# Turning the attention stages' tiles through the vector engine and DRAM instead of the matrix engine, on one Trainium2 core

## The chip, the cores and the metric

The kernel runs on one core of a Trainium2 chip. Five engines work on their own instruction streams: PE (matrix multiplication, with its weight loads shown as PEld), DVE (element-wise work and 32x32 block transposes), ACT (activations and copies), POOL (here powers and the issue of some DMAs) and SP (the issue of most DMAs). The metric is the device time of one execution in microseconds (us); several executions of the same program are compared by their median.

## The reference

One decoder layer over 256 tokens of width 2048, all in float32:

```
h = h + 1/2 * SwiGLU_1(RMSNorm(h))                 # d_ff = 5632
n = RMSNorm(h); P = n @ W_in                       # columns split among head groups
   A: retention, 8 heads of 128 (rotary, decay matrix, per-head GroupNorm, swish gate)
   B: sliding-window attention, 16 query heads on 2 key heads of 64, window 128, rotary, sinks
h = h + concat(A, B) @ W_out
h = h + CrossAttn(RMSNorm(h), RMSNorm(mem))        # 4 heads of 512 into 256 memory tokens
h = h + 1/2 * SwiGLU_2(RMSNorm(h))
out = RMSNorm(h)
```

A sliding head sees, for queries of the first 128 tokens, 128 keys (early groups, t = 0); for those of the second 128 tokens, 256 keys (late groups, t = 1). Softmax has one learned sink per head in its denominator.

## The kernel before

**The stream of weights.** Nearly all of PE's work is `x @ W` for large W. Every weight matrix is cut into `Unit`s (512 output columns, some 256) and each unit into steps. A step is 1024 weight values per partition: two blocks of 128 rows by 512 columns. `split` makes of a float32 weight piece `wf` a rounded part `wh` (ACT, line 71) and the rest `wl` (DVE, line 76), a pair that the text calls a split or halves; `three` (lines 468 to 470) multiplies with three matmuls, high by high, low by high and so on. For two token halves and two row blocks a step has 12 matmuls. All units stand in one list, `all_steps()` makes the order of steps, and `run_stream` writes them out one after another; units with `then` set are interleaved, so that each one's last row block comes after the others.

**Its lead.** At step c, `prepare(at + 1 + LOOKAHEAD)` writes the split of step c + 3, and `fetch(... + AHEAD)` the loads of four steps more. `wf` has three buffers of two steps, `wh` and `wl` have four each.

**Work beside the stream.** Everything else is a task with a due time: `later(delay, fn)` puts it `delay` steps after the current one, and tasks due are written into the program ahead of the split of that step. Each task's instructions stay behind what PE, ACT and DVE have already been given. So a unit's `done` function runs after its last step, and what it starts follows at fixed numbers of steps. `SWA_EVERY = 5` spaces the sliding-head groups, `TURN = 6` is the time of an exchange.

**Two ways to turn a tile.** PE can transpose 128x128 (a matmul with the identity `ident`) into a PSUM tile `tmp` (four of one bank), from which ACT and DVE make the halves. The other way is `cross`: DVE transposes 32x32 blocks of two 128x512 tiles into a `t4k` tile (two buffers), SP writes it to a DRAM `box` one step later, POOL reads it back with the blocks exchanged in four DMAs two steps after the start, and after six steps the function given to it uses the turned tile. In the kernel before, `cross` serves the feed-forward activations, the retention's queries and keys, all outputs that are added to h, and the memory attention's queries and keys.

**The mixer**, in the order of its units: sliding keys and values (`skv`, 4 steps), sliding queries (`sq`, two units of 8), then for each half g of the retention heads queries, keys (`rqk`), values (`rv`) and gate (`rg`), 8 steps each, then four units of `w_out` over the four blocks of `mixT`: blocks 0 and 1 are the retention's, 2 and 3 the sliding heads'. It is followed by the memory attention's keys, queries, values and output, four units each.

In the mixer before, PE turns: the keys (line 597), the queries (line 694, high and low parts side by side), each group's probabilities five steps after its scores (line 644), the gated retention output (line 334) and, later, the memory attention's probabilities (line 901). A sliding-head group (`swa_group`) is four early or two late heads. Its scores take one matmul per head against the keys' high and low halves side by side (line 618), and two DVE instructions add them with scale and mask (lines 623, 624). Then come maximum, exponential (ACT, line 633), sum and product (line 637). `swa_values` (four steps after the probabilities' halves) multiplies with the values and writes its part of `mixT` 2 and 3.

## Time and profile before

| | |
|---|---|
| three runs | 2184.91, 2185.42, 2190.97 us; median 2185.42 |
| profiled execution | 2186.15 us, its span from first to last instruction 2184.4 |
| granted PE clock | 0.999 |
| DVE, ACT, POOL busy | 1290.9, 1028.1, 135.4 us |
| moved by DMA | 472.00 MB, mean 216 GB/s |

In a row of the profile, `L644 PE MATMUL tmp<-ident,t2k 128*128 128x128 f32 x48 | 7.2, 272 | 0.0` is a line of the kernel, the engine, the operation, output and inputs by their names in the program, shapes and count; then busy us, mean ns of one, and the engine's idle time ahead of them with what ended it. In a timeline a row begins with start and duration in us. Matmuls overlap in PE's pipeline, so that the length of one is more than it takes from the stream; the distance from start to start shows the latter.

### The profile page before, as it was taken

The page shows a single profiled execution, that of the slowest core. Times are in us where ns is not written, and L with a number is a line of the kernel's source. Part 1 is how long each engine was busy: PE and PEld are TensorE (multiplying, and loading weights), DVE is VectorE, ACT ScalarE, POOL GpSimd, SP SyncE. Part 2 cuts the span into 40 slices and gives each one's busy share as a digit, 9 for nine tenths or more (in the row PEclk, how much of TensorE's full clock was granted, in tenths as well). Part 3 has the DMA queues.
Part 4 walks back from the last instruction along what each step waited for, and adds up shares of the span by engine and source line. Part 5 has one row for each costly group of instructions (what it writes and reads, how often), then busy time and mean ns, then how long its engine had stood idle before and what let it go on. Part 6 is the DMA issues. An engine that isn't in the chain of part 4 may idle for free.

```text
span 2184.4 us, 25213 instructions
## 1 busy us (share of the span) xinstructions
PE 2171.3 (99%) x9844; PEld 1803.3 (83%) x9844; DVE 1290.9 (59%) x1536; ACT 1028.1 (47%) x1258; POOL 135.4 (6%) x233
## 2 busy tenths in 40 slices
PE   9999999999999999999999999999999999999998
PEld 7888888888888888888888888888888888888886
DVE  6555555555556678786765555575555544555554
ACT  6444444444445555544654444455444433444443
POOL 0000000000000000000111000010101000000000
PEclk9999999999999999999999999999999999999999
DMA  7666677666667656556777655585768655666664
GB/s 270 231 218 216 212 231 225 218 212 227 216 224 254 216 175 199 179 183 205 269 238 246 216 174 174 202 258 201 256 232 255 214 193 193 212 211 213 221 212 145
DMA packets 134745, 472.00 MB, mean 216 GB/s; under 512 B 11233, under 2 KB 12001, under 8 KB 134497
## 3 DMA queue, kind: packets, MB, share of 16 engines
q1 hardware_dynamic: 123968, 441.88, 58.5%
q0 software_dynamic: 10368, 28.33, 5.5%
q8 instruction: 77, 1.26, 0.2%
q14 instruction: 44, 0.35, 0.0%
q10 hardware_dynamic: 288, 0.18, 0.0%
HBM read 439.93 MB, written 30.41 MB: 215 GB/s over the span
## 4 chain that ended last, share of the span: by engine, by line
PE 95%; DVE 2%; issue 2%; DMA 1%; ACT 0%; POOL 0%; SPq 0%; POOLq 0%; ACTq 0%; DVEq 0%
PE acc L469 31%; PE acc L468 31%; PE acc L470 31%; DVE wl L76 1%; PE tmp L470 0%; PE tmp L469 0%; PE tmp L468 0%; DMA t4k<-box 0%; DMA wf<-in_ffn_w_up 0%; PE tmp L618 0%; PE tmp L644 0%; ACT wh L71 0%; POOL t4k L455 0%; PE tmp L740 0%; DVE t4k L446 0%
## 5 line engine op out<-in xcount | busy, mean ns | idle before, releaser
L76 DVE TENSOR_TENSOR wl<-wf,wh 128x1024 fp32r<-128x1024 f32 (+1 forms) x776 | 942.2, 1217 | 789.9 <-ACT wh L71 787.1
L71 ACT ACTIVATE wh<-wf 128x1024 fp32r<-128x1024 f32 (+1 forms) x776 | 817.5, 1055 | 983.8 <-PE acc L470 947.2
L468 PE MATMUL acc<-wh,blk 128*128 128x512 f32 (+1 forms) x3104 | 1207.3, 389 | 2.3 <-ACT blk L71 2.3
L469 PE MATMUL acc<-wl,blk 128*128 128x512 f32 (+1 forms) x3104 | 1205.4, 388 | 0.4 <-DVE wl L76 0.4
L470 PE MATMUL acc<-wh,blk 128*128 128x512 f32 (+1 forms) x3104 | 1204.7, 388 | 0.0
L468 PEld LDWEIGHTS acc<-wh,blk 128*128 128x128 f32 x3104 | 582.9, 188 | 122.3 <-ACT blk L71 2.9
L470 PEld LDWEIGHTS acc<-wh,blk 128*128 128x128 f32 x3104 | 582.8, 188 | 120.4 <-DVE blk L356 0.4
L469 PEld LDWEIGHTS acc<-wl,blk 128*128 128x128 f32 x3104 | 582.9, 188 | 119.9 <-DVE wl L76 1.8
L455 POOL DMA_DIRECT2D t4k<-box x216 | 124.7, 584 | 1759.9 <-DMA box<-t4k 1034.6
L446 DVE STREAM_TRANSPOSE t4k<-t2k 128x512 f32<-128x512 f32 x76 | 49.3, 687 | 13.9 <-ACT t2k L71 13.9
L71 ACT ACTIVATE blk<-t4k 128x512 fp32r<-128x512 f32 (+1 forms) x68 | 39.1, 623 | 34.0 <-DMA t4k<-box 34.0
L76 DVE TENSOR_TENSOR blk<-t4k,blk 128x512 fp32r<-128x512 f32 x60 | 38.7, 687 | 14.5 <-ACT blk L71 14.4
L505 ACT ACTIVATE t2k<-acc,n 128x512 f32<-128x512 f32 x44 | 27.9, 686 | 31.2 <-PE acc L470 31.2
L71 ACT ACTIVATE blk<-tmp 128x512 fp32r<-128x512 f32 (+2 forms) x53 | 23.9, 458 | 25.0 <-DVE blk L76 19.6
L512 DVE SCALAR_TENSOR_TENSOR t2k<-acc,n,t2k 128x512 f32<-128x512 f32 x44 | 31.0, 746 | 6.4 <-PE acc L470 6.4
L71 ACT ACTIVATE blk<-h,gains 128x256 fp32r<-128x256 f32 x64 | 27.3, 496 | 1.5 <-DVE h L479 1.4
L356 DVE SCALAR_TENSOR_TENSOR blk<-h,gains,blk 128x256 fp32r<-128x256 f32 x64 | 26.8, 477 | 0.0
L76 DVE TENSOR_TENSOR blk<-tmp,blk 64x256 fp32r<-64x256 f32 (+2 forms) x45 | 22.1, 494 | 5.2 <-ACT blk L71 5.1
L393 DVE TENSOR_TENSOR t2k<-t2k,t2k 128x512 f32<-128x512 f32 x35 | 24.0, 687 | 1.5 <-ACT t2k L389 0.3
L479 DVE TENSOR_TENSOR h<-h,t4k 128x512 f32<-128x512 f32 x32 | 20.6, 685 | 4.1 <-DMA t4k<-box 4.1
L468 PE MATMUL tmp<-blk,blk 128*128 128x256 f32 (+1 forms) x80 | 22.6, 282 | 0.0
L469 PE MATMUL tmp<-blk,blk 128*128 128x256 f32 (+1 forms) x80 | 22.5, 282 | 0.0
(125 smaller groups left out, 460.3 us busy)
## 6 DMA issues: line engine op xcount, KB each, us to landing
wf<-in_ffn_w_down SPq DMA_DIRECT2D x88, 1024.0 KB, 4.8
wf<-in_ffn_w_gate SPq DMA_DIRECT2D x87, 1024.0 KB, 5.1
wf<-in_ffn_w_up SPq DMA_DIRECT2D x87, 1024.0 KB, 5.5
box<-t4k SPq DMA_DIRECT2D x54, 512.0 KB, 3.2
t4k<-box POOLq DMA_DIRECT2D x216, 128.0 KB, 5.1
wf<-in_w_in_rqk SPq DMA_DIRECT2D x16, 1024.0 KB, 5.1
wf<-in_w_in_rvg SPq DMA_DIRECT2D x16, 1024.0 KB, 5.2
wf<-in_w_out SPq DMA_DIRECT2D x16, 1024.0 KB, 5.0
```

Source lines behind the costliest of these rows:

```text
L71: return nc.scalar.activation(dst, src, AF.Copy, **kw)
L76: nc.vector.tensor_tensor(lo, src, hi, ALU.subtract)
L356: nc.vector.scalar_tensor_tensor(x[:, k, 1, :], v[:, k, :], g, x[:, k, 0, :], ALU.mult, ALU.subtract)
L393: nc.vector.tensor_tensor(self.sums, self.sums, y, ALU.add)
L446: nc.vector.transpose(z[:, t, :].rearrange("p (g q j) -> p q g j", g=4, q=4), squares_of(v))
L455: nc.gpsimd.dma_start(z[32 * g : 32 * g + 32].rearrange("p t (i n) -> p (t i) n", i=4), far[g])
L468: nc.tensor.matmul(o, ah, bh, start=start, stop=False)
L469: nc.tensor.matmul(o, ah, bl, start=False, stop=False)
L470: nc.tensor.matmul(o, al, bh, start=False, stop=stop)
L479: nc.vector.tensor_tensor(v, v, out[t], ALU.add)
L505: nc.scalar.activation(gated[b][t], acc[:, t, :], AF.Silu, scale=norm.scale(t))
L512: nc.vector.scalar_tensor_tensor(s[t], acc[:, t, :], norm.scale(t), s[t], ALU.mult, ALU.mult)
```

## The change

- The queries, the sliding heads' and the memory attention's probabilities and the gated retention output go through `cross` instead of PE. Only the keys are still turned by PE. The helper `turn` and the rounded identity `identr` are gone.
- The sliding queries are rotated into two `t2k` tiles and exchanged; the halves are made after the exchange (one pair for each token half and each of even and odd heads) and the high part lies on partitions 0 to 63 of `q`, the low on 64 to 127, as before.
- Sliding-head groups of one kind go in pairs: `swa_pair` runs two groups five steps apart, and the second one starts an exchange of both probability tiles. The values follow three (or four) steps after it.
- For late groups, the products with the keys' high and low halves are accumulated in PSUM (two matmuls of 256 columns per head), and one DVE instruction adds scale and mask.
- The retention's halves are made per token half and block of 128 columns, with the gain.
- The memory's norm blocks start from the second gate unit instead of the first `w_out` unit; `w_out` takes its blocks in the order 0, 2, 3, 1, and its first two units are interleaved.

```diff
-    def swa_group(g, t, heads, q, probs):
+    def swa_group(g, t, heads, q):
...
-        for b in range(2):
+        if t == 1:
+            ps = tmp_ps().rearrange("p (n k) -> p n k", n=nh)
+            for n in range(nh):
+                for c in range(2):
+                    nc.tensor.matmul(
+                        ps[:, n, :], q[:, heads[n], P:], st["k"][:, g, c, :], start=c == 0, stop=c == 1
+                    )
+            mask = ctab[:, C_MASK : C_MASK + S].rearrange("p (o k) -> p o k", o=1).broadcast_to([P, nh, S])
+            nc.vector.scalar_tensor_tensor(sv3, ps, 64 ** -0.5, mask, ALU.mult, ALU.add)
+        for b in range(0 if t == 1 else 2):
...
-        def second():
-            tp = tmp_ps()
-            for n in range(4):
-                nc.tensor.transpose(tp[:, n * P : (n + 1) * P], s[:, n * P : (n + 1) * P], ident)
...
-        later(5, second)
+        return s
+
+    def swa_pair(g, t, groups, q):
+
+        ss = []
+
+        def group(heads):
+            ss.append(swa_group(g, t, heads, q))
+            if len(ss) == 2:
+                cross(ss, second)
+
+        def second(out):
+            x = blk().rearrange("p k c s -> p k (c s)").rearrange("p k (n s) -> p k n s", n=4)
...
+            if t == 0:
+                for j in range(2):
+                    later(3 + j, lambda j=j: swa_values(g, t, groups[j][-1] // 4, pairs[j : j + 1]))
+            else:
+                later(3, lambda: swa_values(g, t, groups[0][-1] // 4, pairs))
+
+        for heads in groups:
+            st["swa_at"] = max(st.get("swa_at", 0) + SWA_EVERY, clock[0] + 1)
+            later(st["swa_at"] - clock[0], lambda heads=heads: group(heads))
...
     def sq_done(g):
         def done(acc):
...
-            z = blk().rearrange("p k c s -> p (k c s)").rearrange("p (t n c d) -> p t n c d", t=2, n=8, c=2)
             q = blk().rearrange("p k c s -> p (k c) s")
+            rs = [t2k() for _ in range(2)]
...
-            later(5, lambda: turned(0))
-            later(6, lambda: turned(1))
+            def turned(out):
+
+                for t in range(2):
+                    for odd in range(2):
+                        hi, lo = (
+                            q[64 * c : 64 * c + 64, odd::2, t * P : (t + 1) * P].rearrange("p n (a j) -> p n a j", a=4)
+                            for c in range(2)
+                        )
+                        halves(hi, lo, out[t][64 * odd : 64 * odd + 64])
+                swa_pair(g, 0, (range(0, 4), range(4, 8)), q)
+                for b in range(2):
+                    swa_pair(g, 1, (range(4 * b, 4 * b + 2), range(4 * b + 2, 4 * b + 4)), q)
+            cross(rs, turned)
...
-            def turned():
-                tp = turn(lambda t, kk: ret[t][:, kk * P : (kk + 1) * P])
-                mixT[g] = split_turned(tp, G_GN + 4 * g)
-            later(3, turned)
+            def turned(out):
+                x = blk()
+                for t in range(2):
+                    for k in range(4):
...
+                        copy(hi, out[t][:, k], scale=g1)
+                        nc.vector.scalar_tensor_tensor(lo, out[t][:, k], g1, hi, ALU.mult, ALU.subtract)
+                mixT[g] = x
+            cross(ret, turned)
+            if g == 1:
+                for b in range(4):
+                    later(4 + 4 * b, lambda b=b: mem_block(b))
...
-    to_h(a["w_out"], mixT, 1.0, (2, 3, 0, 1), None, out_done)
+    to_h(a["w_out"], mixT, 1.0, (0, 2, 3, 1), None, out_done)
+    units[-4].then = units[-3]
...
-        def probs():
-            tq = tmp_ps()
...
-        later(3, probs)
+        def probs(out):
+            w = blk().rearrange("p k c s -> p k (c s)")
...
+        if i % 2 == 0:
+            st["p"] = p
+        else:
+            cross([st["p"], p], probs)
```

## The prediction

> **What bounds the kernel now.** I read the page's busy times and its chain first, then the matrix engine's groups with shapes kept apart, then the starts of single instructions around the transposes, and last the vector engine where it is fullest.

> ```profile
> span 2184.4 us, 25213 instructions
> PE 2171.3 (99%) x9844; PEld 1803.3 (83%) x9844; DVE 1290.9 (59%) x1536; ACT 1028.1 (47%) x1258; POOL 135.4 (6%) x233
> PEclk9999999999999999999999999999999999999999
> PE 95%; DVE 2%; issue 2%; DMA 1%; ACT 0%; POOL 0%; SPq 0%; POOLq 0%; ACTq 0%; DVEq 0%
> ```

> PE is busy for 99% of the span at full clock and is 95% of the chain that ended last. Every instruction in PE's stream is therefore time, and what leaves the stream is gained unless PE then waits for something. The instructions that the change takes out are these (mean ns is of one, overlapped):

> ```profile
> L644 PE MATMUL tmp<-ident,t2k 128*128 128x128 f32 x48 | 7.2, 272 | 0.0
> L618 PE MATMUL tmp<-blk,blk 128*128 128x512 f32 x16 | 5.2, 408 | 0.0
> L694 PE MATMUL tmp<-identr,blk 128*128 128x128 f32 x32 | 3.2, 244 | 0.0
> L901 PE MATMUL tmp<-ident,t2k 128*128 128x128 f32 x16 | 2.4, 271 | 0.0
> L334 PE MATMUL tmp<-ident,t2k 128*128 128x128 f32 x16 | 2.1, 272 | 0.0
> ```

> L644 turns the sliding heads' probabilities, L694 their queries, L901 the memory attention's probabilities, L334 the retention output: 48 + 32 + 16 + 16 = 112 transposes. L618 makes the scores and stays.

> **What leaves PE.** A transpose's 272 ns is latency. What it takes from the stream is read from the chain (start, us, what) and from the starts of neighbouring instructions:

> ```profile
> 769.87 0.23 PE acc L469
> 776.91 0.64 PE tmp L694 x8
> 780.36 0.47 PE tmp L618 x4
> 795.17 0.47 PE tmp L618 x2
> 795.63 0.44 PE tmp L644 x4
> 899.97 0.87 PE tmp L334 x8
> 1273.10 0.44 PE tmp L901 x4
> ```
> ```profile
> 795.47 0.60 PE L644 MATMUL tmp<-ident,t2k 128*128 128x128 f32 x4
> 795.83 0.48 PE L468 MATMUL acc<-wh,blk 128*128 128x512 f32 x1
> 796.14 0.40 PE L469 MATMUL acc<-wl,blk 128*128 128x512 f32 x1
> ```

> By the chain: 12 x 0.44 + 4 x 0.64 + 2 x 0.87 + 4 x 0.44 = 5.3 + 2.6 + 1.7 + 1.8 = 11.4 us. By starts, four L644 take 0.36 (795.47 to 795.83), and the next matmul's gap is 0.31 instead of 0.23. Where a score group stands just ahead, that 0.08 may stay, so the lower end is 12 x 0.36 + 6.1 = 10.4. I take 10.7, since most L644 groups run behind L618. The late scores (16 matmuls of 512 columns, 0.47 for two) become 32 of 256 columns (0.47 for four): no change. Nothing is added to PE's stream.

> [...]

> **What is added to DVE.** Twelve new exchanges (2 of queries, 6 of probability pairs, 2 of retention, 2 of memory attention), each with two block transposes:

> ```profile
> 942.65 1.31 DVE L446 STREAM_TRANSPOSE t4k<-acc 128x512 f32<-128x512 f32 x2
> 943.99 0.69 DVE L76 TENSOR_TENSOR t2k<-tmp,t2k 128x512 fp32r<-128x512 f32 x1
> 944.60 0.74 DVE L623 SCALAR_TENSOR_TENSOR t2k<-tmp,ctab 128x256 f32<-128x256 f32 x2
> 945.26 0.74 DVE L624 SCALAR_TENSOR_TENSOR t2k<-tmp,t2k 128x256 f32<-128x256 f32 x2
> 848.68 0.17 DVE L630 TENSOR_SCALAR nmx<-m 128x2 f32<-128x2 f32 x1
> L727 DVE TENSOR_TENSOR t2k<-t4k,ctab 64x512 f32<-64x512 f32 x8 | 5.5, 687 | 0.3
> ```

> Start to start, a pair of transposes takes 1.34, a 512-wide operation 0.61, a 256-wide one 0.33. So +12 x 1.34 = 16.1. The eight late groups make their scores in one 512-wide instruction from PSUM (0.67, as two of 0.33) instead of four of 0.33: -8 x 0.66 = -5.3. The queries' split is made twice as often (8 halves over 64 partitions for 4): +4 x 0.61 = 2.4. Retention's split goes from 8 of 256 columns to 16 of 128 (0.2 each), the memory probabilities' from 4 of 512 to 8 of 256: +0.5 together. DVE gains 13.7 of 1290.9 us and stays far below PE in total; ACT's copies change as little. What counts is the mixer, where DVE is full:

> ```profile
> 790.00:860.00 70.00, 70.00 (x342) 58.41 (x341) 59.96 (x105) 37.82 (x67) 4.64 (x8) 1.00 0.63 206
> 920.00:970.00 50.00, 49.81 (x236) 41.17 (x236) 42.63 (x77) 24.99 (x46) 4.65 (x8) 1.00 0.57 185
> ```

> The columns are us, then PE, PEld, DVE, ACT and POOL busy: DVE 86% and 85%. The cover is that weights are split three steps before use (LOOKAHEAD = 3; a step is 12 matmuls of 0.23, 2.7 us). It ends where much DVE work falls between two splits:

> ```profile
> 828.08 1.22 DVE L76 TENSOR_TENSOR wl<-wf,wh 128x1024 fp32r<-128x1024 f32 x1
> 836.74 1.22 DVE L76 TENSOR_TENSOR wl<-wf,wh 128x1024 fp32r<-128x1024 f32 x1
> 839.74 0.40 PE L469 MATMUL acc<-wl,blk 128*128 128x512 f32 x1
> 956.65 1.23 DVE L76 TENSOR_TENSOR wl<-wf,wh 128x1024 fp32r<-128x1024 f32 x1 [0.70 <-ACT wh L71]
> 966.45 1.21 DVE L76 TENSOR_TENSOR wl<-wf,wh 128x1024 fp32r<-128x1024 f32 x1
> 967.13 0.39 PE L468 MATMUL acc<-wh,blk 128*128 128x512 f32 x1
> 967.71 0.50 PE L469 MATMUL acc<-wl,blk 128*128 128x512 f32 x1 [0.19 <-DVE wl L76]
> ```

> 8.7 us without a split (836.74) left 839.74 - 837.96 = 1.8 of slack; 9.8 us (966.45) made PE's next matmul start 0.58 after the last instead of 0.23. That 0.35 is PE's only stall in the mixer today. Both are places where the retention's rotary work (eight instructions of L727's kind, bars of 0.69, some 5.3 us start to start) meets a sliding-head group.

> I count steps from the first one of the mixer and write out the due times by hand. Before, rotary work falls due at steps 34, 42, 66, 74, and the groups at 18, 23, 28, ... 73, so at 33 and 73 a step ahead of it. After, the query exchange takes six steps instead of five, the groups fall due at 19, 24, ... 74, and every second one ends in its exchange. Three places get fuller:
> - Step 34: late group (scores 0.67, reduction 0.61, six small ones of 0.17 at most, 0.6, product 0.61), its transposes 1.34, rotary 5.3, the values' split 0.67, a table product 0.61: 10.4 us in one step. Between the two splits above lay 8.66 - 1.22 = 7.4, with 1.8 of slack left. PE is given 1.2 more in that step (scores 0.47, six value matmuls of 256 columns 0.7): 3.0 more work against 3.0 of cover. Stall 0 to 1.8, and I take a third, 0.6.
> - Step 74: 9.1 (the same without values and table) where 9.8 - 1.22 = 8.6 lay, with the slack already 0.35 short and PE given 0.47 more: stall 0 to 1.8 (as at 34), I take 0.8.
> - Steps 18 to 20: the queries' split 2.4, an early group 3.2, then rotary of the second queries 3.8 and transposes 1.34. Carrying over what a step leaves, with each step's own split of 1.2, 8.4 us stand there at step 20, for 6.2 before. The same carrying gives 8.0 at steps 34 and 74 of before, the verge. Stall 0 to 3, I take 0.6, near the low end as the verge is; the upper end comes from late data, next.

> **The exchange's latency.** A turned tile is now used six steps (16.3 us) after its exchange begins.

> ```profile
> ACT blk L71 <- DMA t4k<-box: 34.0, 26, 3.9
> SPq L450 <- DVE t4k L446: 242.7, 52, 8.2
> box<-t4k SPq DMA_DIRECT2D x54, 512.0 KB, 3.2
> t4k<-box POOLq DMA_DIRECT2D x216, 128.0 KB, 5.1
> L455 POOL DMA_DIRECT2D t4k<-box x216 | 124.7, 584 | 1759.9 <-DMA box<-t4k 1034.6
> L772 POOL TENSOR_TENSOR gnr<-gnv,mhalf 128x4 f32<-128x4 f32 x4 | 4.1, 1016 | 78.0 <-DVE gnv L771 78.0
> ```

> Write 3.2, four issues 2.3, landing 5.1: 10.6 us after the transposes. They come behind a rotary or softmax chain, 5 to 9 us into the step, so data land 16 to 20 us after it: ACT waits 0 to 4 us at the split, as it does 26 times today (up to 3.9) without PE noticing. Behind that wait on ACT are the weight copies, and DVE behind them. With three steps of cover I take it as free, except at step 18, where a wait of 3 us would push the pile at step 20 over: the 3 above.

> SP: twelve more writes, each waiting for its transposes ahead of weight loads (8.2 us at most today). A load is issued four steps (10.9 us) before its split and lands in 5.1, and the split stands 3 steps ahead: a hold under some 11 us is hidden. POOL: 48 more issues, 28 us on an engine busy 6%; the four powers (L772) may stand behind reads for 0 to 2.3 us each, hidden by the four steps until their use. Buffers: at most two exchanges are open at any due time, which is what t4k has. DMA traffic grows by 12 x 1 MB, written and read.

> w_out: block 1 (the second retention group) is made at step 90 instead of 87 and used at 96, as its first two units are interleaved; blocks 2 and 3 are complete at 83, used from 86. The memory's norm blocks come eleven steps earlier into a stretch with one DVE block less: nothing.

> **Sum.** -10.7 (PE) + 0.6 + 0.8 + 0.6 (new stalls) - 0.35 (the old one, replaced) + 0.2 (small waits) = -8.9. The profiled execution took 2186.15 us (span 2184.4 and 1.75 around it), so 2177.3 by it; it stands 0.7 above the median of the runs, 2185.42, from which I forecast 2176.5.

> **Rivals.**
> - The piles eat most of it. The three upper ends give 1.8 + 1.8 + 3, and one more place (steps 49 and 54, where a group meets the retention halves or another exchange) 0 to 2. So 3.5 to 9 us come back: 2179 to 2185. For it: DVE at 85% and a stall already there. Against: one stall of 0.35 in 240 us.
> - Slower: the box writes hold SP. It decides where a hold exceeds 11 us: each of the 12 writes then delays a weight load, and PE stands for the excess. At 13 us of hold it is 2 x 12 = 24, net +13: 2198. For it: 8.2 today, and at steps 34 and 74 the transposes come 9 to 10 us late. Against: the write is queued a step after its exchange, so the hold is 7 there.
> - The transposes cost what their bars show and nothing comes back: 48 x 0.272 + 32 x 0.244 + 16 x 0.271 + 16 x 0.272 = 29.6, so 2155.8. For it: the groups' mean ns. Against: in 0.36 us four of them start and PE's next matmul follows.
> - No change: the stretch is DVE's, not PE's, so PE only waits longer. That is the first rival in full, 2184 to 2186.

> **How the numbers follow.** Forecast 0.58, piles 0.31, SP 0.07, bars 0.02, more than the forecast's gain (no stall at all, 11.4) 0.02. 0.3% is 6.6 us, about what a measurement of this kernel can tell; faster by that means below 2178.9. That holds the forecast, the bars and the fuller gain: 0.62. Within: the piles, 0.31. Slower: 0.07. The range goes from the full 11.4 with the old stall gone (2173.7) to the piles' end, 2185.

> **What would show it.** Right: L644, L694, L901 and L334's groups gone from PE, its count down by 96 (112 less, 16 score matmuls more), about 10.7 us less in its stream; 66 box writes for 54 and 264 reads for 216; PE's waits on wl, if any, near the rotary work at steps 34 and 74 and after step 20, each under 2 us. Wrong: PE waits of over 4 us in sum, waits of ACT's wh on a weight load (SP held), or PE's spacing changed where nothing was removed.

## The result, and the profile after

| | median, us | lowest to highest | ratio to before, 95% interval |
|---|---|---|---|
| before (beside it, 4 runs) | 2185.74 | 2184.91 to 2190.97 | |
| after (4 runs) | 2205.09 | 2198.93 to 2208.72 | 1.0080 [1.0065, 1.0095] |

The change makes the kernel slower by 17.5 us (0.8% of 2185.7). The ratio, here and below, is estimated from all the runs and is not the quotient of the two medians, which with four runs each are rough (they differ by 19.4 us). The forecast was 2176.5, and the time lies outside its range. The profiled execution took 2204.57 us.

The page of the changed kernel: busy times, the chain, and median landing times of DMAs (last number, us).

```profile
PE 2170.9 (99%) x9748; PEld 1798.4 (82%) x9748; DVE 1302.6 (59%) x1551; ACT 1026.7 (47%) x1266; POOL 164.8 (7%) x281
PE 85%; DMA 6%; DVE 5%; issue 2%; ACT 1%; POOL 1%; SPq 0%; ACTq 0%; POOLq 0%; DVEq 0%
box<-t4k SPq DMA_DIRECT2D x66, 512.0 KB, 3.2
t4k<-box POOLq DMA_DIRECT2D x264, 128.0 KB, 5.9
wf<-in_w_in_rqk SPq DMA_DIRECT2D x16, 1024.0 KB, 9.2
wf<-in_w_in_rvg SPq DMA_DIRECT2D x16, 1024.0 KB, 8.6
```

PE's 96 instructions less, the 66 writes and the 264 reads are as forecast. The page still says that PE is busy for 99%: this share hides the loss. The chain shows it: PE holds 85% of it where it held 95%, and DMA and DVE have 11% for 3%. And the weights of the mixer land in 9 us. Before, these two rows read:

```profile
wf<-in_w_in_rqk SPq DMA_DIRECT2D x16, 1024.0 KB, 5.1
wf<-in_w_in_rvg SPq DMA_DIRECT2D x16, 1024.0 KB, 5.2
```

The next view says what PE stood for (us in total, times, longest).

```profile
PE tmp L452 <- ACT blk L71: 5.2, 3, 2.4
PE acc L453 <- DVE wl L76: 4.7, 6, 1.5
PE tmp L388 <- DVE t2k L385: 3.2, 2, 2.7
PE tmp L744 <- DVE blk L735: 2.5, 1, 2.5
PE tmp L611 <- DVE blk L76: 1.6, 1, 1.6
PE tmp L453 <- DVE blk L76: 1.3, 4, 0.5
PE tmp L745 <- DVE blk L735: 1.1, 1, 1.1
```

Rows on `tmp` are PE's own attention work: sliding values (L452, L453 on `tmp`), scores (L611), the retention's scores (L744, L745) and a norm's sum (L388). Only 4.7 us are waits of the weight stream for `wl`. Before, from 720 to 1120 us, there was this and no more:

```profile
PE tmp L404 <- DVE t2k L401: 0.5, 1, 0.5
PE acc L469 <- DVE wl L76: 0.2, 1, 0.2
```

So most stalls stand at PE's attention work and not in the weight stream. The values and the first scores use newly exchanged tiles (5.2 + 1.6 + 1.3 = 8.1 us), a place for which the prediction had no term of its own. The retention's scores (3.6 us) use tiles that were exchanged before too; they wait in the kernels below without late tiles as well.

What ACT and SP wait for in the changed kernel, in this order (ACT from 720 to 1120 us, the mixer and w_out; SP in the whole execution):

```profile
ACT wh L71 <- DMA wf<-in_w_in_rvg: 31.3, 7, 9.1
ACT wh L71 <- DMA wf<-in_w_in_rqk: 15.2, 6, 4.7
ACT blk L71 <- DMA t4k<-box: 11.1, 8, 3.0
```
```profile
SPq L434 <- DVE t4k L430: 299.4, 58, 15.6
SPq L434 <- DVE t2k L748: 39.1, 2, 23.5
```

Before, SP's longest hold by a box write was 8.2 us, and 5.3 in this stretch; ACT waited there for no weights and for no turned tile. In the whole execution ACT waits for turned tiles 57.2 us in 37 places after and 34.0 in 26 before, but the others of these belong to the feed-forwards and the memory attention. All three of the prediction's signs of "wrong" are there: PE waits of over 4 us in sum, `wh` waiting on a load, and PE's spacing, to which the clock comes below.

Two pieces of the chain of waits show a tile being late (start, us, what). The first is the first queries' exchange, the second a pair of late probabilities:

```profile
771.45 0.70 DVE t4k L430
...
772.18 3.11 DMA box<-t4k
...
775.87 0.60 POOL t4k L439
776.47 6.63 DMA t4k<-box
```
```profile
986.77 0.19 DVE t2k L749
986.96 0.61 DVE t2k L630
...
987.59 0.71 DVE t4k L430
...
988.33 3.21 DMA box<-t4k
...
992.11 1.72 POOL t4k L439 x3
993.82 7.78 DMA t4k<-box
...
1001.71 0.42 ACT blk L71
...
1003.30 0.33 PE tmp L453
```

From the last transpose to the landing it takes 11.0 us (772.15 to 783.10) in one and 13.3 in the other (988.30 to 1001.60), where the prediction had 10.6. In the second, DVE comes to the transposes only after the products of the retention's scores with the decay matrix (L749) and the softmax product (L630), and PE starts on the values the moment that the halves are made. A third piece shows SP's queue:

```profile
801.59 0.07 SPq L434
...
801.76 6.39 DMA wf<-in_w_in_rqk
...
808.25 1.07 ACT wh L71
...
809.35 1.24 DVE wl L76
...
810.63 0.50 PE acc L453
```

The write (L434) leaves SP only when its transposes are done; the weight load behind it leaves next, lands 6.4 us later, and its split is what PE waits for.

**The clock.** After four of its waits, the two longest among them (starts 3.13 and 2.87 us apart), PE is slow for a while. The timeline of PE around one of these (start, duration, instruction, idle time before it):

```profile
871.58 0.70 PE L744 MATMUL tmp<-blk 128*128 128x256 f32 x2 [2.48 <-DVE blk L735]
...
875.38 0.63 PE L454 MATMUL acc<-wh,blk 128*128 128x512 f32 x1
875.81 0.63 PE L452 MATMUL acc<-wh,blk 128*128 128x512 f32 x1
...
878.00 0.40 PE L452 MATMUL acc<-wh,blk 128*128 128x512 f32 x1
878.23 0.39 PE L453 MATMUL acc<-wl,blk 128*128 128x512 f32 x1
```

Start to start it is 0.43 us instead of 0.23, half speed, for some 3 us; the granted clock is 0.51 from 874.1 to 877.6. Counted over all matmuls after the first 100 us (starts 0.19 to 0.215 us further apart than 0.2265 for 512 columns, and in proportion for the smaller ones), this costs 7.4 us after and 1.9 before, where the granted clock of the mixer is 1.00 and the wider starts have another reason. So 5.5 of the loss are not waits at all, but what follows them: four stretches at half clock.

**Where it is lost.** The 9312 matmuls of the weight stream are the same in all kernels, so the start of the n-th can be compared. The table gives the difference to before in us, set to zero at n = 3300, where the mixer begins (one profiled execution each, for no_dma and traffic the fastest, 4.1 and 2.0 us below their medians; the kernels of the other columns are those of the experiments):

```
   n  before at   after  no_dma hold_only traffic pairs_pe  best2
3600    823.6     -1.4    -4.5    -2.6     -3.2     +1.0    -2.0
3900    906.8     +6.4    -4.4    +1.8     -1.9     +4.5    -3.4
4200    988.5    +10.1    -7.8    -1.6      0.0     +3.8    -3.2
4500   1057.4    +16.3    -7.3     0.0     +3.1     +4.3    -2.8
4800   1127.2    +20.2    -7.3    -0.3     +3.1     +9.7    -2.3
5100   1195.2    +20.2    -7.3    -0.3     +3.1     +9.7    -2.3
5700   1353.5    +18.2    -9.2    -2.2     +1.2     +7.8    -4.2
```

All of the loss is in the mixer and w_out. In the memory attention every kernel of the table gains 1.9, the 16 transposes of L901 (forecast 4 x 0.44 = 1.8), with no new wait.

### The profile page after: what moved, and what is told of

Read it like the earlier page. It is cut to its first block, busy times and chain, and to the rows that moved or that the text cites. A ratio compares the mean times of both kernels' runs of the same rounds, so it can differ in the third digit from the quotient of the medians.

```text
span 2202.7 us, 25187 instructions
## 1 busy us (share of the span) xinstructions
PE 2170.9 (99%) x9748; PEld 1798.4 (82%) x9748; DVE 1302.6 (59%) x1551; ACT 1026.7 (47%) x1266; POOL 164.8 (7%) x281
## 4 chain that ended last, share of the span: by engine, by line
PE 85%; DMA 6%; DVE 5%; issue 2%; ACT 1%; POOL 1%; SPq 0%; ACTq 0%; POOLq 0%; DVEq 0%
PE acc L452 28%; PE acc L453 28%; PE acc L454 28%; DMA t4k<-box 2%; DVE wl L76 2%; DMA wf<-in_w_in_rvg 1%; DMA wf<-in_ffn_w_up 1%; ACT wh L71 1%; DMA blk<-in_mem 1%; POOL t4k L439 0%; PE tmp L453 0%; PE tmp L454 0%; PE tmp L452 0%; DVE t4k L430 0%; DVE blk L76 0%
## 5 line engine op out<-in xcount | busy, mean ns | idle before, releaser
L76 DVE TENSOR_TENSOR wl<-wf,wh 128x1024 fp32r<-128x1024 f32 (+1 forms) x776 | 940.7, 1217 | 782.9 <-ACT wh L71 779.5
L71 ACT ACTIVATE wh<-wf 128x1024 fp32r<-128x1024 f32 (+1 forms) x776 | 815.0, 1055 | 970.8 <-PE acc L454 896.3
L453 PE MATMUL acc<-wl,blk 128*128 128x512 f32 (+1 forms) x3104 | 1208.0, 389 | 4.7 <-DVE wl L76 4.7
L452 PE MATMUL acc<-wh,blk 128*128 128x512 f32 (+1 forms) x3104 | 1208.7, 389 | 2.2 <-ACT blk L71 1.4
L453 PEld LDWEIGHTS acc<-wl,blk 128*128 128x128 f32 x3104 | 584.5, 188 | 126.2 <-DVE wl L76 7.6
L452 PEld LDWEIGHTS acc<-wh,blk 128*128 128x128 f32 x3104 | 584.5, 188 | 122.8 <-ACT blk L71 2.3
L439 POOL DMA_DIRECT2D t4k<-box x264 | 152.4, 584 | 1814.5 <-DMA box<-t4k 1153.9
L71 ACT ACTIVATE blk<-t4k 128x512 fp32r<-128x512 f32 (+3 forms) x104 | 54.1, 572 | 56.8 <-DMA t4k<-box 56.8
L430 DVE STREAM_TRANSPOSE t4k<-t2k 128x512 f32<-128x512 f32 x100 | 65.9, 690 | 14.0 <-ACT t2k L71 13.8
L76 DVE TENSOR_TENSOR blk<-t4k,blk 128x512 fp32r<-128x512 f32 (+2 forms) x96 | 55.6, 619 | 27.1 <-ACT blk L71 26.7
L452 PE MATMUL tmp<-blk,blk 128*128 128x256 f32 (+1 forms) x88 | 25.4, 289 | 5.2 <-ACT blk L71 5.2
L71 ACT ACTIVATE blk<-h,gains 128x256 fp32r<-128x256 f32 x64 | 27.3, 495 | 3.2 <-DVE h L463 3.2
L453 PE MATMUL tmp<-blk,blk 128*128 128x256 f32 (+1 forms) x88 | 25.6, 291 | 1.3 <-DVE blk L76 1.3
L626 ACT ACTIVATE t2k<-t2k,nmx 128x128 f32<-128x128 f32 (+1 forms) x32 | 14.2, 446 | 26.1 <-DVE nmx L623 20.2
L454 PE MATMUL tmp<-blk,blk 128*128 128x256 f32 (+1 forms) x88 | 25.6, 290 | 0.0
## 6 DMA issues: line engine op xcount, KB each, us to landing
box<-t4k SPq DMA_DIRECT2D x66, 512.0 KB, 3.2
t4k<-box POOLq DMA_DIRECT2D x264, 128.0 KB, 5.9
```

Source lines behind the costliest of these rows:

```text
L71: return nc.scalar.activation(dst, src, AF.Copy, **kw)
L76: nc.vector.tensor_tensor(lo, src, hi, ALU.subtract)
L430: nc.vector.transpose(z[:, t, :].rearrange("p (g q j) -> p q g j", g=4, q=4), squares_of(v))
L439: nc.gpsimd.dma_start(z[32 * g : 32 * g + 32].rearrange("p t (i n) -> p (t i) n", i=4), far[g])
L452: nc.tensor.matmul(o, ah, bh, start=start, stop=False)
L453: nc.tensor.matmul(o, ah, bl, start=False, stop=False)
```

## The experiments

The theories that the expectations refer to: (1) box writes hold SP's queue and with it the weight loads; (2) an exchange takes longer than its six steps, and PE's own tasks wait for it; (3) DVE's added work; (4) ACT, in order, stands at a late tile with weight copies behind it; (5) the added traffic slows the weight loads. All medians are beside runs of the kernel before on the same chip (2185.6 to 2186.2); a difference in us worked out below is one of ratios times 2185.7. The interval of such a difference, worked out as the root of the sum of both squares, is some 3 us on either side between kernels of eight to eleven runs and 4 to 5 us where one of them has four or five.

**no_dma.** `new` marks the twelve new exchanges; their block transposes are made and the halves read them directly.

```diff
-        later(1, write)
-        later(2, read)
+        if not new:
+            later(1, write)
+            later(2, read)
```

> The changed kernel, in which the twelve new exchanges keep their block transposes on DVE and their due times, but neither write the box nor read it back: the halves are made from the tile that was not exchanged (so the attention results are of the wrong elements). DVE's, ACT's and PE's instructions stay. Theory 1 (the box writes wait in SP's queue for late transposes and hold the weight loads behind them) and theory 2 (an exchange through DRAM takes longer than its six steps, and PE's own tasks wait for it): both expect nearly all of the 27 us of new PE waits gone, 2176 to 2182 us. Theory 3 (DVE has 14 us more to do where it was 85% full): 2192 to 2205 us, as after the change.

2180.5 us (2176.36 to 2183.27), 0.9975 [0.9965, 0.9986]. PE's two longest waits after the start-up:

```profile
PE tmp L745 <- DVE blk L736: 1.7, 1, 1.7
PE tmp L746 <- DVE blk L736: 1.1, 1, 1.1
```

DVE does all that the change gives it (busy 1301.9 us, after 1302.6), and the loss is gone. So theory 3 is not the cause of the loss; that lies in the way through DRAM.

**pool_write.** The new exchanges' writes leave from POOL's queue.

```diff
-            nc.sync.dma_start(box.rearrange("(t p) n -> p t n", t=2), z)
+            (nc.gpsimd if new else nc.sync).dma_start(box.rearrange("(t p) n -> p t n", t=2), z)
```

> The changed kernel, with the box writes of the twelve new exchanges issued from POOL's queue, ahead of their reads there, instead of SP's. Theory 1: SP is held no more than in the kernel before, weight loads land in 5 us again, the stalls on weights (about 6 us) and a part of the late reads go: 2188 to 2195 us. Theory 2: reads land no sooner than the transposes allow, PE's waits on late halves stay: 2198 to 2204. Theory 3: unchanged, 2200 to 2206.

2199.74 us, 1.0063 [1.0048, 1.0078]. ACT's waits on the mixer's weights fall from 46.5 to 8 us, and its waits on turned tiles there rise from 11.1 to 17.9. So the holds that theory 1 names are real, but taking them away gives only 3.7 us, which is not clear of noise.

**due_shift** and **pool_due.** Values, retention scores and retention values two steps later, the first group one; in pool_due with POOL's writes as well.

```diff
-                    later(3 + j, lambda j=j: swa_values(...
+                    later(5 + j, lambda j=j: swa_values(...
...
-                later(4 + i // 2, lambda i=i: ret_scores(g, i, qk))
+                later(6 + i // 2, lambda i=i: ret_scores(g, i, qk))
```

> The changed kernel, in which what PE does with turned tiles falls due later: the sliding values five steps (five and six for the early pair) after the halves instead of three, the retention scores six after the keys instead of four, with the two retention halves two steps later as well, the very first group one step later. Writes stay on SP. Theory 2: PE's waits on late halves and rotary output (about 14 us with the slower clock after them) go: 2186 to 2192. Theory 1: the stalls on weights stay and late reads are as late, 2194 to 2201. Theory 3: the same work on DVE, 2198 to 2205.

> Both edits: box writes of the new exchanges from POOL's queue, and the later due times for PE's tasks on turned tiles. Theories 1 and 2 together: the waits go but for a few us, 2176 to 2182, below the kernel before. Theory 3: 2192 or more.

2201.41 us, 1.0078 [1.0061, 1.0095], and 2204.99 us, 1.0085 [1.0070, 1.0100]: nothing gained, against the expectation. The waits changed place. This is the top of pool_due's list for PE and then, from 720 to 1120 us, for ACT:

```profile
PE acc L453 <- DVE wl L76: 8.5, 6, 3.5
PE tmp L388 <- DVE t2k L385: 5.0, 1, 5.0
```
```profile
ACT blk L71 <- DMA t4k<-box: 38.0, 8, 9.0
```

Giving PE's tasks more time does not make the tile earlier. ACT stands up to 9 us at its first use, longer than the three steps (8 us) by which the weight copies behind it are ahead, and PE waits for `wl` instead. That is theory 4; where it is the tile that is late, only the exchange's own time can help.

**turn8** and **turn8_pool.** So the new exchanges get eight steps, three `t4k` buffers and, so that w_out finds its blocks, block 0 of both first units first.

```diff
+        if new:
+            delay = 8
...
-        z = work.tile([P, 2, 512], F32, tag="t4k", name=nm("t4k"), bufs=2)
+        z = work.tile([P, 2, 512], F32, tag="t4k", name=nm("t4k"), bufs=3)
```

> The changed kernel with eight steps instead of six for the twelve new exchanges, from their start to the use of the turned tile on ACT and DVE. A third t4k buffer pays for the longer lives (t2k has six buffers for seven, the small statistics four for eight), and w_out's first two units both take block 0 first, since the sliding blocks come two to three steps later. Writes stay on SP. Theory 4 (an exchange takes longer than six steps, ACT then waits at the head of its in-order queue, and the weight copies behind it come late): ACT's waits on turned tiles fall to the level of the kernel before, 2180 to 2188 us. Theory 1 (writes hold SP, the loads behind are late): little changes, 2196 to 2203. Theory 5 (the added DRAM traffic itself slows the weight loads): 2196 to 2203.

> The eight-step kernel with the box writes of the new exchanges issued from POOL's queue. Theories 1 and 4 together: weight loads land in 5 to 6 us, ACT waits little, 2176 to 2183 us, below the kernel before. Theory 5: 2193 or more.

2197.01 us, 1.0047 [1.0030, 1.0065], and 2194.2 us, 1.0038 [1.0023, 1.0052]. 7.2 and 9.2 us are back, less than theory 4 expected. In the profile of the first, ACT waits in the mixer for only one turned tile, 0.3 us, as theory 4 has it; but it waits 38.4 us for weights there, SP is held up to 21.8, and PE stands 6.3 us for `wl`. The longest of these waits (3.6) comes after 8.8 us without a split on DVE (834.8 to 843.6), where a late load, rotary work, three block transposes and a group's scores now meet. In the profile of the second, one wait for a late tile makes PE's starts 6.7 us apart (971), and the norm's sum 3.5 (1067). Other due times make other meetings on DVE and SP, so giving the tiles more steps does not measure what their lateness costs.

**pairs_pe** and **mem_psum.** Parts of the change: all but the probabilities of the sliding heads, which PE turns again; and the kernel before with only the memory attention's exchange and the late scores in PSUM.

```diff
-                cross(ss, second)
+            later(5, lambda: one(j, s))       # four PE transposes per group, halves as in the change
```

> The changed kernel with the sliding heads' probabilities turned by PE again (48 transposes, five steps after each group's scores, values four steps later); queries, retention and memory attention still go through DRAM, six steps each. If the six pair exchanges cause the waits (theories 1, 4 and 5 alike, half of the exchanges and those in the fullest stretch): 2180 to 2188 us. If the queries', the retention's or the earlier memory blocks cause them: 2197 to 2207.

> The kernel before with two parts of the change alone: the memory attention's probabilities through DRAM in pairs (16 PE transposes less, about 1.7 us) and the late sliding scores accumulated in PSUM (no PE time, DVE 5 us less where it is fullest, where PE stood for 0.35 us). All theories on the waits: the memory stage has DVE, SP and DMA to spare, 2182.5 to 2185 us. If any exchange through DRAM costs waits wherever it stands: 2187 or more.

2190.21 us, 1.0017 [1.0008, 1.0026], and 2182.99 us, 0.9986 [0.9977, 0.9995]. Without the probabilities' six exchanges 13.8 of the 17.5 us are gone, though these take the most transposes off PE (48). The parts of mem_psum are a gain. The rest (queries, retention, w_out's order, the memory's place) loses 6.8 against it.

**hold_only** and **traffic.** no_dma had taken away writes, reads and lateness together. In hold_only the new exchanges are written by SP and not read; in traffic they are also read by POOL in the same pieces at the same step, but into another DRAM tile that nobody waits for.

```diff
         later(1, write)
-        later(2, read)
+        later(2, copy_box if new else read)     # traffic; in hold_only: nothing if new
```

> The changed kernel with the twelve new exchanges written to DRAM by SP but not read back (the halves are made from the block-transposed tiles, so the output is not the reference's). The late writes still stand ahead of weight loads in SP's queue, but no turned tile is late. Theory 1 (the held queue alone is the loss): as slow as the change, about 2203 to 2205, with ACT's weight copies waiting some 45 us on loads and PE's waits near those of the change. Theory 2 (the tiles' lateness is the loss, the hold alone is covered by the lead of the weights): 2180 to 2182, as where neither is done (2180.5), although SP waits on the transposes as long as before. Between: the queue's share is the time less 2180.5; from the writes moved to POOL's queue, which gained 5.4, I expect up to 2186.

> The changed kernel with the twelve new exchanges written by SP as in the change and their boxes read by POOL in the same pieces at the same step, but into another DRAM tile that nothing waits for; the halves are made from the block-transposed tiles (the output is not the reference's). All the writes, holds and reads are there, no turned tile is late. Lateness theory (2 and 4): within 2 us of the version with writes alone, 2182 to 2186. Traffic theory (5): the weights land later with the reads beside them, their median landing stays near 9 us and PE waits for wl as in the change: 2195 to 2205.

2183.78 us, 0.9990 [0.9979, 1.0000], and 2187.66 us, 1.0008 [0.9998, 1.0017]. The traffic kernel's waits of PE after the start-up, then those of ACT and SP, and its landings:

```profile
PE acc L459 <- DVE wl L76: 4.9, 7, 2.0
PE tmp L750 <- DVE blk L741: 2.1, 1, 2.1
PE tmp L751 <- DVE blk L741: 2.0, 2, 1.1
PE tmp L388 <- DVE t2k L385: 0.5, 1, 0.5
```
```profile
ACT wh L71 <- DMA wf<-in_w_in_rvg: 29.1, 8, 10.0
ACT wh L71 <- DMA wf<-in_w_in_rqk: 16.5, 7, 5.8
```
```profile
SPq L434 <- DVE t4k L430: 298.2, 58, 17.0
```
```profile
wf<-in_w_in_rqk SPq DMA_DIRECT2D x16, 1024.0 KB, 7.7
wf<-in_w_in_rvg SPq DMA_DIRECT2D x16, 1024.0 KB, 8.6
```

The rows of ACT and SP are nearly those of the change: SP is held as long, ACT waits for weights as long (45.6 for 46.5), the loads land nearly as late (7.7 and 8.6 for 9.2 and 8.6). And yet the kernel is 15.7 us faster than the change. PE waits as long as there for `wl` (4.9 for 4.7) and for the retention's scores (4.1 for 3.6); what is gone is the 8.1 us at the sliding values and first scores and 2.2 of the norm's sum, and there is one stretch of half clock (at 941.8) for four. So the ladder is

| step | ratio | adds, us |
|---|---|---|
| transposes gone, DVE's work there (no_dma) | 0.9975 | |
| writes that hold SP (hold_only) | 0.9990 | 3.3 |
| as many bytes read (traffic) | 1.0008 | 3.9 |
| tiles that are waited for (after) | 1.0080 | 15.7 |

The first two additions are each hardly larger than their uncertainty (3 us on either side); the third is far outside. The traffic kernel reads into DRAM and not into the SBUF tile, so its traffic is near the change's but not the same.

**mem_late.** The change with the memory's loads two steps earlier, used at the same step, and the norm's sum two steps later.

```diff
-                    later(4 + 4 * b, lambda b=b: mem_block(b))
+                    later(2 + 4 * b, lambda b=b: mem_block(b))
...
-        later(3, made)
+        later(5, made)
...
-    nmem = Norm(G_MEM, "nmem", 4)
+    nmem = Norm(G_MEM, "nmem", 6)
```

> The changed kernel with the memory's loads two steps earlier, their norm blocks at the same step as before, and the norm's sum two steps later. Theory: in the change the loads of the memory land late (7.9 to 11.2 us) in ACT's order and the sum of squares then lets PE stand (2.7 us at 1077, 2.4 at 1037) and its clock go to half (another 1 to 2): these go, 2199 to 2201. Rival: it is the first output exchange, not the memory's load, that DVE waits for ahead of the sum: then the stall at 1037 goes and the one at 1077 stays, 2202 to 2204. Neither, if PE's waits only move: 2205.

2197.35 us, 1.0053 [1.0038, 1.0067]: 5.9 us are back, more than expected. At the sum, PE's starts are 0.94 apart instead of 3.13, without the half clock after it, and the waits at 1037 are gone (one of 1.1 stands at 1019). The memory's new place, priced at nothing, cost a stall; but not by itself, for in hold_only and traffic the memory stands at the same place and the sum waits 0.2 and 0.5 us.

**ret_mem.** mem_psum with the retention's exchange.

> The kernel before with the memory attention's probabilities and the gated retention output through DRAM and the late scores added in PSUM; queries and sliding probabilities stay on PE, w_out and the memory's blocks as before. 16 transposes less than in the version without the retention (2183.0), by the chain 1.7 us: 2181.3 if the six steps and the place in the list of steps cover the exchange; the second retention block is due two steps ahead of its use. Rival: that block comes late and PE waits for its halves in w_out, 1 to 3 us: 2182.5 to 2185.

2185.26 us, 0.9995 [0.9985, 1.0006]. Between n = 3300 and 4800 its profile gains 1.1 us more than mem_psum's, of the 1.7 expected. The total is not faster, because of waits for `wl` from 1546 to 1685 us, in the second feed-forward, where the two kernels have the same instructions. Why some executions have these, I can't say; the run doesn't settle the retention's worth.

**best** and **best2.** pairs_pe with POOL's writes, seven steps for the queries and mem_late; best2 also starts the first group one step later and takes block 0 of both first w_out units first.

```diff
-            cross(rs, turned)
+            cross(rs, turned, 7, new=True)
...
-            st["swa_at"] = max(st.get("swa_at", 0) + SWA_EVERY, clock[0] + 1)
+            st["swa_at"] = max(st.get("swa_at", 0) + SWA_EVERY, clock[0] + 2)      # best2
```

> The changed kernel with the sliding probabilities back on PE, the writes of the remaining new exchanges on POOL's queue, the queries' exchange with seven steps, and the memory's loads two steps earlier with the norm's sum two steps later. 64 transposes are off PE (6.1 us by the chain: 16 x 0.16 of queries in eights, 1.74 of retention, 1.76 of memory). Theory 2 with the stat stall: against the version with only the probabilities put back (2190.2), the wait of the first scores (2.2), the sum's stall with its half clock (3.1 + 2.4) and one or two waits for wl (1.5 to 3) go: 2180 to 2183. Rival: the waits for wl in the mixer stay, since DVE and ACT have the exchanges' work and the weights in one order: 2185 to 2187.

> The version with sliding probabilities on PE, POOL's writes, seven steps for the queries and the later memory sum, and here also the first group two steps after the queries' halves for one, and the first block of both w_out units ahead of the second block of either. If the first scores' wait on the halves (2.3 us in the profile of the version without this) is on the path: 2 us less than that version, about 2181. Rival: the wait moves to the next user of a late tile or to wl: no difference, 2183 to 2184.

2183.19 us, 0.9988 [0.9980, 0.9997], and 2181.43 us, 0.9979 [0.9970, 0.9988]. What PE waits for in best2, after the start-up:

```profile
PE tmp L391 <- DVE t2k L388: 1.0, 1, 1.0
PE tmp L657 <- ACT wh L71: 0.7, 1, 0.7
```

The wait of the first scores on the halves is gone and the median is as expected, but the two ratios' intervals overlap, and best2 has a second edit. In the profiles best2 is 1.8 us ahead of best at n = 3600, after the first scores, and 0.3 at n = 4800; whether that wait was on the path is not shown. best2 beats before and after. Against mem_psum (0.9986) the intervals overlap.

## Why the prediction was wrong

- **PE's work.** Right in the profile. By the stream's matmuls the profiled no_dma is 9.2 us ahead of before, with 2.8 us of waits at the retention's scores in it. The forecast was 10.7 less 1.8 of stalls. The transposes cost the stream what starts and chain said, not their bars. But that execution was no_dma's fastest, with a granted clock of 0.999; the other seven had 0.997 to 0.998, and by the ratio no_dma gains 5.5 us (3.1 to 7.7), less than the 8.9 of the sum.
- **DVE's piles** (0.6 + 0.8 + 0.6): 2.8 us of waits are left with the exchanges' DRAM part away, near the 2.0 of the forecast, but by luck: they stand at the retention's scores and not at the split of weights, for which the piles were worked out.
- **"With three steps of cover I take it as free."** This is the step that failed. The wait itself was forecast well: ACT waits for new tiles in the mixer in 8 places, 3.0 us at most (forecast 0 to 4). What was wrong is that it is free. The precedent was misread: of the 26 waits "without PE noticing" of the kernel before, none stands in the mixer. And the cover is the weights', made three steps ahead. Values come three steps after their halves, but the first scores only one, and while ACT stands at a tile the weight copies behind it lose their cover too (a wait of 2.55 us at the turned queries ends at 783.18, and the weight copy behind them starts at 784.24 with no wait of its own). Priced at 0 (3 at step 20), it cost 15.7, with the half clock after the waits and the memory's place in it. That the difference lies in the waiting is shown by the traffic kernel, as far as its reads into DRAM stand for those into SBUF; which share is the tiles' own lateness and which the copies behind them was not separated.
- **"A hold under some 11 us is hidden", "the hold is 7 there".** The hold was taken from the kernel before (8.2, and that outside the mixer). The ten new writes of the mixer held SP for 3.1 to 23.5 us, six of them for more than 11, since the transposes come behind other work on DVE; the traffic kernel has the same 23.5 without late tiles. The rival that the writes hold SP (chance 0.07, 2198) named a thing that happened and came nearest to the total, the latter by luck: by its own rule the six would cost 32 us (the sum of what exceeds 11), and the holds measured 3.3 (hold_only) and 3.7 (pool_write), with 3 and 5 on either side.
- **DMA traffic** was named with its bytes and without a price: 3.9 us, with 3 on either side.
- **"The memory's norm blocks ...: nothing."** The cover named (one DVE block less) was not what counted: the load landed 7.9 to 11.2 us after its issue (6.2 before, by the median), ahead of weight copies on ACT, and the sum met the first output exchange. 5.9 us, with 5 on either side, and only beside late tiles.
- The sum lacked the half clock after four of the waits: 5.5 us of the profile.
- The range of the first rival (2179 to 2185) is about 1 us above its own terms: 2185.4 - 10.7 + 3.5 to 9 gives 2178 to 2184. Neither holds the measured time.

## What to carry to other kernels

Turning a tile by another engine and DRAM trades throughput on the full engine (here 5.5 us, by no_dma) for latency (here 11.0 and 13.3 us from the last transpose to the landing), so count steps from when the source is really ready to when the first engine that uses the tile needs it, and don't count on the cover of another stream. When tasks wait in an in-order queue (a write in SP's, a copy in ACT's), ask what stands behind them; here moving the consumer later only moved the wait there (ACT's 11.1 us at turned tiles in the mixer became 38.0 in pool_due, where POOL writes as well). To split such a loss, make the work without the dependence: the same writes, holds and reads with nothing waiting on them.

## What the runs showed of the hardware

The loads of the same 1 MB of weights landed in 5.1 and 5.2 us before, 5.2 and 6.5 with DVE's added work alone (no_dma), 7.1 and 7.7 with the writes, 7.7 and 8.6 with the reads too, by the median. Held loads leave close together (in the change, three within 3.4 us after the write at 881.9); whether it is this or the exchange's transfers beside them that makes them land later was not separated.
